# The opening of a conditioned decoder layer: c by DMA broadcast, eight early conditioning tiles, and a new order and pacing of the first weight pieces

## The chip, the cores and the metric

The kernel runs on one core of one Trainium2 chip. The metric is device time in microseconds for one execution, and for several runs their median. A core has TensorE (PE, matmuls), VectorE (DVE), ScalarE (ACT), GpSimd (POOL) and SyncE (SP, which here only issues DMAs); 16 DMA engines move data between HBM and the on-chip memory. Every engine works through its own queue in the order in which the program issued the instructions, and waits at an instruction until its inputs and its output buffer are ready.

## The reference, cut to what matters

One decoder layer on x (256 tokens by 2048) with a conditioning vector c (2048). Only the start of it is touched by the change:

```python
mod = (silu(c) @ w_cond + b_cond).reshape(B, 3, 3, 2048)
u = x * (1 + mod[:, 0, 1]) + mod[:, 0, 0]            # scale and shift of sub-layer 0
h = (silu(u @ ffn1_w1) * (u @ ffn1_w3)) @ ffn1_w2    # F = 5632
x = layer_norm(2**0.25 * x + 0.5 * (1 + mod[:, 0, 2]) * h)
...                                                  # mixer (attention | S5), then a second FFN
```

All values are fp32. w_cond has 9 x 2048 rows of 2048 numbers (75 MB), of which the scale and shift of the first FFN are 2 x 2048 rows.

## The kernel before, in words

**Conditioning pieces.** silu(c) lies in the tile `sc`, the same row on all 128 partitions. One *piece* is a tile `gv` of 128 rows by 1024 columns of w_cond (512 KB, `gv_load`, issued on SP at L211); `gv_step` multiplies it with half of `sc` on DVE and sums along the row into one column of `acc`. Four pieces (two blocks, shift and scale, by two halves) give the shift and scale for 128 columns of u, a *k-tile*. There are 16 k-tiles, grouped into four *units* of four; a unit is 16 pieces, so the first FFN needs 64 pieces (0 to 63), and later blocks the rest of 288. `gv` has four buffers (`GVB`), and a step loads up to three pieces ahead.

`finish` turns the sums into scale and shift (four small DVE operations); `modulate` makes the k-tile of u: ACT writes `uf` = scale * x + shift, then `Uh` (its rounded part, on ACT or DVE) and `Ul` = uf - Uh (DVE). For the first unit `finish` runs after every fourth piece; for later units, once after the sixteenth, through `gv_end`. x itself comes transposed in tiles `xT`, one per unit (`load_xT`).

**Weight pieces and jobs.** The FFN's weights come as tiles `raw` of 128 x 1024 (512 KB). A `Stream` holds a list of *jobs*, one weight piece each. For job j ACT writes hi(j) = rounded raw (`S.copy` in `split_to`), DVE writes lo(j) = raw - hi(j) (in `pay`), and PE multiplies in 12 matmuls of 512 columns (`form_b`): for each of two token tiles, hi with Uh and Ul of two k-tiles, then lo with Uh of both. `hi` and `lo` have four buffers each (`AHEAD`), `raw` four, of which three are used ahead from job 4 to job 51 (`RW`).

`Stream.run` issues, for each job, in this order: the job's `pre` functions, the matmuls, its `post` functions, what `later` has put on this job, the splits up to job j + `AHEAD` (ACT's hi and DVE's lo of job j + 4), and the job's background `bg`.

**The first 80 jobs** form u @ (w1 | w3) for five blocks b of 512 columns, for w1 and w3 (m = 0, 1), in four passes over k: pass i uses unit i. In each pass a block and m take two jobs, each with two k-tiles, so a pass has 20 jobs and starts at job 0, 20, 40, 60. The first job of each pass has in its `pre` a `gv_until`, which makes pieces until the unit is ready and then makes its four k-tiles of U at once. Blocks 0 to 3 are evicted from PSUM after each pass: in pass 0 by two ACT copies into a tile `kosum` per block and m (L909), in later passes by two DVE additions; block 4 stays in PSUM.

**The opening** (the end of `tile_layer`): c goes to one partition, four pairs of fp32 matmuls with a row of ones broadcast it into PSUM, and four Silu on ACT write `sc`. All 16 pieces of the first unit are made; the loads of the first weight pieces are slipped in after pieces 8 and 12 (`W0_AT`, the `NK` test), hi(0) after piece 13, and lo(0) to lo(3) after the last. Then the jobs run. Their background makes pieces up to a count that depends on the job:

```python
for i in range(4 * NT1):
    n = min(64, NK + math.ceil(min(i + 1, GA[0]) * GA[1] + max(0, i + 1 - GA[0]) * GA[2]))
    stream.q[i].bg.append(lambda n=n: steps(n - gv_n["done"]))
```

with GA = (20, 0.9, 0.8) and NK = 16. `lam_prep`, a chain of small DVE operations on four 64-vectors (`lamv`), is done after job 2. From job 80 on a planner (`drain`), which counts estimated PE and DVE time, puts the remaining pieces and the S5 preparation between the jobs.

Of the kernel before, what the change touches and what calls it, by code (L numbers as in the profile page):

```python
# [16 lines left out]
D = 2048  # L17
# [10 lines left out]
NSLAB = 12  # L28
GVB = 4
CH = 1024  # L30
DL = 2
DP = 0
RAW = 4
# [4 lines left out]
XA = 16  # L38
W0_AT = 12
S0_AT = 13  # L40
LIM = (2.6, 100.0, 100.0, 100.0)
# [3 lines left out]
GV_END = 256  # L45
GA = (20, 0.9, 0.8)
UNITS = ([("p", 0, q) for q in range(4)] + [("g", 2, h) for h in range(2)] + [("p", 3, q) for q in range(4)]
# [70 lines left out]
def tile_layer(tc, A, out):  # L118
    nc = tc.nc
    V, S, PE, SP, GP = Meter(nc.vector), nc.scalar, Meter(nc.tensor), nc.sync, nc.gpsimd  # L120
    with ExitStack() as ctx:
# [8 lines left out]
        def psum():  # L130
            return psp.tile([128, 512], F32, tag="ps", name="ps")
# [7 lines left out]
        def w1(shape, name):  # L139
            return small(shape, name, 5, tag="w1")  # L140
# [23 lines left out]
        sizes = {k: int(np.prod(v)) for k, v in shapes.items()}  # L164
        cst = sb.tile([128, sum(sizes.values())], F32, tag="cst", name="cst")
        SP.dma_start(cst, A["cst"])
        view, o = {}, 0
# [4 lines left out]
        bcT, lngT, lnbT, s5a, s5d, glub, sublng = (view[k] for k in shapes)  # L172
        lamv = w1([128, 4, 64], "lamv")
        SP.dma_start(lamv, A["lamv"].rearrange("(o a) b -> o a b", o=1).to_broadcast([128, 4, 64]))
        sc = sb.tile([128, D], F32, tag="sc", name="sc")
        SP.dma_start(sc[0:1, :], A["c"])
        ones = w1([1, 128], "ones")
        V.memset(ones, 1.0)
        for q in range(4):
            p = psum()  # L180
            PE.matmul(p, ones, sc[0:1, q * 512:(q + 1) * 512], start=True, stop=True)
            S.activation(sc[:, q * 512:(q + 1) * 512], p, AF.Silu)  # L182
        lam = sb.tile([128, 1], F32, tag="lam", name="lam")
# [7 lines left out]

        st = {"raw": RAW, "lim": None, "gv_max": 0.0, "gv_credit": 0.0, "s5_at": 0.0}

# [8 lines left out]
        def gv_load(k):  # L202
            while gv_n["load"] < min(k, len(gv_order), gv_n["cap"]):
                n = gv_n["load"]
                (kind, blk, i), j = gv_order[n]
                if kind == "p":
                    col, half = (blk + j % 2) * NK + 4 * i + j // 4, j // 2 % 2
                else:
                    col, half = blk * NK + 8 * i + j // 2, j % 2
                t = gvp.tile([128, 1024], F32, tag="gv", name="gv", bufs=GVB)  # L210
                SP.dma_start(t, A["w_cond"][col, :, half * 1024:(half + 1) * 1024])  # L211
                gv_tiles[n] = t, half
                gv_n["load"] += 1
# [391 lines left out]

        def lam_prep():
            pr = w1([128, 2, 64], "lampr")
            V.tensor_tensor(pr, lamv[:, 0:4:2, :], lamv[:, 1:4:2, :], op=ALU.mult)
            sm, ex = small([128, 2], "lams", 1), small([128, 2], "lame", 1)
            V.tensor_reduce(sm, pr, axis=AX.X, op=ALU.add)  # L610
            vexp(V, ex, sm, cells(w1([128, 256], "lamc")), 2)
            V.tensor_tensor(lam, ex[:, 0:1], ex[:, 1:2], op=ALU.subtract)
            V.tensor_scalar(lam, lam, LAMBDA_INIT, None, op0=ALU.add)


        class Stream:
# [43 lines left out]
            def run(self, n):  # L660
                for _ in range(n):
# [12 lines left out]
                    if not j.hold:  # L674
                        self.split_to(self.done + AHEAD)
                        for f in j.bg:
                            f()
                        drain()
# [200 lines left out]
        def ffn(w13, wd, blk, passes, tiles, kept):  # L879
# [138 lines left out]
            for i, (k0, k1) in enumerate(passes):  # L1018
                n = len(jobs)
                for b in range(tiles // 4):  # L1020
                    kps = range(k0 // 2, k1 // 2)
                    if (i, b) == (0, 0):
                        jobs += [mk_ko(i, b, m, kp) for kp in kps for m in range(2)]
                    else:
                        jobs += [mk_ko(i, b, m, kp) for m in range(2) for kp in kps]
                jobs[n].pre.append(lambda k0=k0, k1=k1: [gv_until("ready", blk, q) for q in range(k0 // 4, k1 // 4)])
            for pi, (f0, nf) in enumerate(PIECES):
# [414 lines left out]

        stream.limit = 0
        gv_load(2)
        load_xT(0)
        for n in range(NK):
            gv_step()
            if n + GVB == W0_AT:
                stream.limit = 10 ** 6
                stream.load_to(1)  # L1450
                stream.limit = 1
            if n + GVB == NK:
                stream.limit = 10 ** 6
                stream.load_to(RAW)
                gv_n["cap"] = len(gv_order)
            if n == S0_AT:
                stream.split_to(1, False)
        pay_late()
        stream.flush()
        stream.pay()  # L1460
        stream.split_to(AHEAD)
        for i in range(4 * NT1):
            n = min(64, NK + math.ceil(min(i + 1, GA[0]) * GA[1] + max(0, i + 1 - GA[0]) * GA[2]))
            stream.q[i].bg.append(lambda n=n: steps(n - gv_n["done"]))
# [126 lines left out]
```

## Time and profile before

| | us |
|---|---|
| runs (3) | median 1926.6, 1925.9 to 1926.9 |
| profiled execution | 1923.86 |
| its span, first to last instruction | 1921.6 |
| PE busy | 1853.3 (96%) |
| DVE busy | 1492.8 (78%) |
| ACT busy | 884.1 (46%) |
| DMA over the span | 532.35 MB, 277 GB/s |
| first matmul of the main work | 32.03 |
| start of unbroken matmuls | 40.69 |

All times in the trace count from the span's start. A row of a timeline gives start, duration, engine, line, operation, output tile and input tiles, and the shapes; in brackets stands how long the engine was idle before it and what released it. "x2" means that two instructions in a row were merged. L106 is a helper through which all DVE and PE calls pass, so rows are told apart by their tiles. A matmul's duration overlaps the next one's; the distance of the starts is its price.

### The profile page before, as it was taken

The numbers are of one execution on the slowest core, as the hardware profiler recorded it, in microseconds if no ns is written. First come the engines' busy times: TensorE is split into PE (matmuls) and PEld (weight loads), VectorE is DVE, ScalarE is ACT, GpSimd is POOL, SyncE is SP. The second block draws the span as 40 slices with busy tenths as digits, with TensorE's granted clock in tenths as the row PEclk, the third lists the DMA queues.
The fourth block names the chain that finished last, engine by engine and source line by source line (L and its number), as shares of the span: only waits on it lengthen the run. The fifth ranks groups of instructions, "written<-read, shape, count | busy, mean of one in ns | idle before, by whom it ended". The sixth has DMA issues, their size and how long they took to land.

```text
span 1921.6 us, 25394 instructions
## 1 busy us (share of the span) xinstructions
PE 1853.3 (96%) x9294; PEld 1559.2 (81%) x9294; DVE 1492.8 (78%) x2285; ACT 884.1 (46%) x1201; POOL 65.5 (3%) x119
## 2 busy tenths in 40 slices
PE   3999999999999999999999998999999999999997
PEld 2888887888888788889998886888888888888886
DVE  5999889788779878887998996888866555454568
ACT  2544544654553343544447635544444444334432
POOL 0000000000000000102210000000000000000000
PEclk9999999999999999999999998999999999999998
DMA  8999758998998898798989795998887655565563
GB/s 307 363 363 337 266 193 282 335 318 315 324 336 293 314 334 302 254 348 284 317 280 313 269 335 198 327 356 293 289 279 255 188 185 187 197 215 189 189 234 114
DMA packets 151791, 532.35 MB, mean 277 GB/s; under 512 B 21825, under 2 KB 23281, under 8 KB 150513
## 3 DMA queue, kind: packets, MB, share of 16 engines
q1 hardware_dynamic: 137090, 495.31, 74.5%
q0 software_dynamic: 6512, 23.89, 3.8%
q10 hardware_dynamic: 8064, 11.54, 1.7%
q8 instruction: 73, 1.20, 0.2%
q14 instruction: 52, 0.43, 0.1%
HBM read 513.34 MB, written 17.33 MB: 276 GB/s over the span
## 4 chain that ended last, share of the span: by engine, by line
PE 83%; DVE 9%; DMA 4%; ACT 2%; issue 2%; POOL 0%; SPq 0%; DVEq 0%; ACTq 0%
PE ps L106 83%; DVE lo L106 3%; DVE gv L106 3%; DMA raw<-in_f1w_dram 2%; DVE Y L106 1%; DMA gv<-in_w_cond_dram 1%; DVE cells L106 1%; ACT hi L647 1%; DMA scrB<-tabr 1%; DMA U<-sD 0%; DVE kosum L106 0%; ACT uf L696 0%; DMA raw<-in_f2w_dram 0%; ACT Y L818 0%; DVE st L106 0%
## 5 line engine op out<-in xcount | busy, mean ns | idle before, releaser
L106 DVE TENSOR_TENSOR lo<-raw,hi 128x1024 fp32r<-128x1024 f32 x630 | 766.1, 1221 | 332.5 <-ACT hi L647 328.9
L647 ACT CAST hi<-raw 128x1024 fp32r<-128x1024 f32 x630 | 660.6, 1052 | 705.0 <-PE ps L106 456.4
L106 PE MATMUL ps<-hi,Uh 128*128 128x512 f32 x1472 | 582.0, 395 | 22.7 <-ACT hi L647 21.7
L106 PE MATMUL ps<-hi,Ul 128*128 128x512 f32 x1472 | 576.4, 392 | 0.0
L106 PE MATMUL ps<-lo,Uh 128*128 128x512 f32 x1472 | 457.0, 392 | 8.0 <-DVE lo L106 8.0
L106 DVE SCALAR_TENSOR_TENSOR gv<-gv,sc 128x1024 f32<-128x1024 f32 x288 | 350.7, 1218 | 15.5 <-ACT sc L182 7.8
L106 PEld LDWEIGHTS ps<-hi,Uh 128*128 128x128 f32 x1472 | 278.0, 189 | 84.3 <-ACT hi L647 24.0
L106 PEld LDWEIGHTS ps<-lo,Uh 128*128 128x128 f32 x1472 | 277.5, 189 | 69.0 <-DVE lo L106 10.9
L106 PEld LDWEIGHTS ps<-hi,Ul 128*128 128x128 f32 x1472 | 278.3, 189 | 56.7 <-DVE Ul L106 0.5
L106 PE MATMUL ps<-hi,Hh 128*128 128x512 f32 (+1 forms) x716 | 274.9, 385 | 0.0
L106 PE MATMUL ps<-hi,Hl 128*128 128x512 f32 (+1 forms) x716 | 273.6, 383 | 0.0
L106 PE MATMUL ps<-lo,Hh 128*128 128x512 f32 (+1 forms) x716 | 216.9, 384 | 2.8 <-DVE lo L106 2.8
L106 PEld LDWEIGHTS ps<-lo,Hh 128*128 128x128 f32 x716 | 132.7, 188 | 31.0 <-DVE lo L106 4.7
L106 PEld LDWEIGHTS ps<-hi,Hh 128*128 128x128 f32 x716 | 134.5, 188 | 27.0 <-issue 0.8
L106 PEld LDWEIGHTS ps<-hi,Hl 128*128 128x128 f32 x716 | 134.6, 188 | 26.0
L106 PE MATMUL ps<-Uh,hi 128*128 128x256 f32 x384 | 98.6, 293 | 2.9 <-ACT sT L1076 1.8
L106 PE MATMUL ps<-Ul,hi 128*128 128x256 f32 x384 | 96.4, 288 | 0.2
L106 PEld LDWEIGHTS ps<-Uh,hi 128*128 128x128 f32 x384 | 74.8, 195 | 6.5 <-ACT sT L1076 2.7
L106 PEld LDWEIGHTS ps<-Ul,hi 128*128 128x128 f32 x384 | 74.9, 195 | 1.1 <-DVE Ul L106 1.0
L942 ACT CAST Hh<-ps 128x512 fp32r<-128x512 f32 x44 | 25.8, 587 | 87.6 <-PE ps L106 87.6
L106 DVE TENSOR_TENSOR Hl<-ps,Hh 128x512 fp32r<-128x512 f32 x44 | 30.2, 687 | 32.8 <-ACT Hh L942 32.8
L106 PE MATMUL ps<-Uh,lo 128*128 128x256 f32 x384 | 53.9, 283 | 0.0
(215 smaller groups left out, 1345.6 us busy)
## 6 DMA issues: line engine op xcount, KB each, us to landing
gv<-in_w_cond_dram SPq DMA_DIRECT2D x288, 512.0 KB, 6.7
raw<-in_f1w_dram SPq DMA_DIRECT2D x264, 512.0 KB, 5.9
raw<-in_f2w_dram SPq DMA_DIRECT2D x264, 512.0 KB, 4.7
raw<-in_win_a_dram SPq DMA_DIRECT2D x48, 512.0 KB, 6.2
raw<-in_wout_dram SPq DMA_DIRECT2D x32, 512.0 KB, 5.5
s5m<-scrB POOLq DMA_DIRECT2D x8, 1024.0 KB, 8.8
raw<-in_win_v_dram SPq DMA_DIRECT2D x16, 512.0 KB, 5.2
scrB<-s5f ACTq DMA_DIRECT2D x8, 640.0 KB, 10.6
```

Of the source, the lines that this page charges most:

```text
L106: return f(*a, **k)
L647: S.copy(hi, raw)
L942: S.copy(hh, p)
```

## The change

- c is read from HBM straight into all 128 partitions, in two transfers of 512 KB, and two Silu of 1024 columns work in place; the matmuls with ones go. A Silu on a tile of one column stands ahead of them.
- The first eight pieces (`EARLY`) lie in four of the twelve `slab` tiles instead of the `gv` ring, so that twelve pieces can be under way before the first step.
- Only eight pieces (k-tiles 0 and 1) are made before job 0, and only two jobs are split ahead (`st["split"]`) until job 4. Pieces 8 to 15 are made in the background of jobs 0 to 3, two each; the `pre` of job 4 sees to what is left and restores the distance of four.
- Pass 0 takes blocks 0 and 1 together, and all their jobs of k-tiles 0 and 1 (jobs 0 to 3) before those of k-tiles 2 and 3 (jobs 4 to 7).
- The pieces of the later units are paced by a new formula, counted from job 4.
- `lamv` is loaded after job 2, and its DVE work is put after job 8.

```diff
+EARLY = 8
...
-W0_AT = 12
-S0_AT = 13
...
-GA = (20, 0.9, 0.8)
+GA = (0.9, 0.8)
...
+        sc = sb.tile([128, D], F32, tag="sc", name="sc")
+        for h in range(2):
+            SP.dma_start(sc[:, h * 1024:(h + 1) * 1024], A["c"][:, h * 1024:(h + 1) * 1024].to_broadcast([128, 1024]))
         SP.dma_start(cst, A["cst"])
...
-        lamv = w1([128, 4, 64], "lamv")
-        SP.dma_start(lamv, A["lamv"].rearrange("(o a) b -> o a b", o=1).to_broadcast([128, 4, 64]))
-        sc = sb.tile([128, D], F32, tag="sc", name="sc")
-        SP.dma_start(sc[0:1, :], A["c"])
-        ones = w1([1, 128], "ones")
-        V.memset(ones, 1.0)
-        for q in range(4):
-            p = psum()
-            PE.matmul(p, ones, sc[0:1, q * 512:(q + 1) * 512], start=True, stop=True)
-            S.activation(sc[:, q * 512:(q + 1) * 512], p, AF.Silu)
+        one = w1([128, 1], "one")
+        V.memset(one, 1.0)
+        S.activation(one, one, AF.Silu)
+        for h in range(2):
+            S.activation(sc[:, h * 1024:(h + 1) * 1024], sc[:, h * 1024:(h + 1) * 1024], AF.Silu)
...
-                t = gvp.tile([128, 1024], F32, tag="gv", name="gv", bufs=GVB)
+                if n < EARLY:
+                    if n % 2 == 0:
+                        st["early"] = slab("early")
+                    t = st["early"][:, n % 2 * 1024:n % 2 * 1024 + 1024]
+                else:
+                    t = gvp.tile([128, 1024], F32, tag="gv", name="gv", bufs=GVB)
...
         def lam_prep():
+            lamv = w1([128, 4, 64], "lamv")
+            SP.dma_start(lamv, A["lamv"].rearrange("(o a) b -> o a b", o=1).to_broadcast([128, 4, 64]))
+            stream.later(6, lambda: lam_rest(lamv))
+
+        def lam_rest(lamv):
...
-                        self.split_to(self.done + AHEAD)
+                        self.split_to(self.done + st["split"])
...
-                for b in range(tiles // 4):
+                groups = [(0, 1), (2,), (3,), (4,)] if (i, blk) == (0, 0) else [(b,) for b in range(tiles // 4)]
+                for bs in groups:
                     kps = range(k0 // 2, k1 // 2)
-                    if (i, b) == (0, 0):
-                        jobs += [mk_ko(i, b, m, kp) for kp in kps for m in range(2)]
+                    if i == 0 and bs[0] == 0:
+                        jobs += [mk_ko(i, b, m, kp) for kp in kps for b in bs for m in range(2)]
                     else:
+                        b, = bs
                         jobs += [mk_ko(i, b, m, kp) for m in range(2) for kp in kps]
-                jobs[n].pre.append(lambda k0=k0, k1=k1: [gv_until("ready", blk, q) for q in range(k0 // 4, k1 // 4)])
+                if (i, blk) != (0, 0):
+                    jobs[n].pre.append(lambda k0=k0, k1=k1: [gv_until("ready", blk, q) for q in range(k0 // 4, k1 // 4)])
...
-        stream.limit = 0
-        gv_load(2)
+        gv_load(3)
         load_xT(0)
-        for n in range(NK):
+        gv_load(EARLY)
+        stream.load_to(2)
+        gv_load(EARLY + GVB)
+        for n in range(8):
             gv_step()
-            if n + GVB == W0_AT:
-                stream.limit = 10 ** 6
-                stream.load_to(1)
-                stream.limit = 1
-            if n + GVB == NK:
-                stream.limit = 10 ** 6
-                stream.load_to(RAW)
-                gv_n["cap"] = len(gv_order)
-            if n == S0_AT:
-                stream.split_to(1, False)
         pay_late()
-        stream.flush()
-        stream.pay()
-        stream.split_to(AHEAD)
+        stream.split_to(2)
+        gv_n["cap"] = len(gv_order)
+
+        def second():
+            steps(NK - gv_n["done"])
+            pay_late()
+            st["split"] = AHEAD
+        stream.q[4].pre.append(second)
         for i in range(4 * NT1):
-            n = min(64, NK + math.ceil(min(i + 1, GA[0]) * GA[1] + max(0, i + 1 - GA[0]) * GA[2]))
+            n = 8 + 2 * i + 2 if i < 4 else min(64, NK + math.ceil(min(i - 3, 16) * GA[0] + max(0, i - 19) * GA[1]))
             stream.q[i].bg.append(lambda n=n: steps(n - gv_n["done"]))
```

More of the change, by code (lines that the diff above doesn't have):

```diff
@@ L190, in tile_layer @@
         yD = dram.tile([1024, 4, 64], F32, tag="yD", name="yD")
-        st = {"raw": RAW, "lim": None, "gv_max": 0.0, "gv_credit": 0.0, "s5_at": 0.0}
+        st = {"raw": RAW, "split": 2, "lim": None, "gv_max": 0.0, "gv_credit": 0.0, "s5_at": 0.0}
         gv_order = [(u, kt) for u in UNITS for kt in range(NK)]
```

## The prediction

> **What bounds the kernel now.** I read the page's busy shares first, then stretches of the opening, then TensorE's own timeline.
>
> ```profile
> span 1921.6 us, 25394 instructions
> PE 1853.3 (96%) x9294; PEld 1559.2 (81%) x9294; DVE 1492.8 (78%) x2285; ACT 884.1 (46%) x1201; POOL 65.5 (3%) x119
> ```
>
> TensorE (PE) has work in flight for 1853 of 1922 us. A microsecond is therefore won or lost only where PE stands still. The stretches (columns: length, busy PE, weight loads, DVE, ACT, POOL, granted clock, DMA share, GB/s):
>
> ```profile
> 0.00:10.00 10.00, 4.32 (x5) 1.83 (x6) 0.32 (x2) 2.41 (x3) 1.59 (x9) 1.00 0.69 199
> 20.00:30.00 10.00, 0.00 (x0) 0.00 (x0) 8.45 (x21) 1.01 (x3) 0.00 (x0) 1.00 0.96 323
> 30.00:40.00 10.00, 2.08 (x4) 1.16 (x4) 6.62 (x15) 3.92 (x7) 0.00 (x0) 1.00 0.99 366
> 80.00:100.00 20.00, 20.00 (x90) 16.57 (x89) 18.05 (x31) 12.86 (x18) 0.00 (x0) 1.00 1.02 408
> 100.00:120.00 20.00, 20.00 (x90) 16.57 (x89) 20.00 (x27) 8.38 (x8) 0.00 (x0) 1.00 0.99 362
> ```
>
> PE is nearly idle for 40 us while the DMA engines are almost full, and from then on PE, DVE and DMA are all close to full together. PE's timeline:
>
> ```profile
> 32.03 0.80 PE L106 MATMUL ps<-hi,Uh 128*128 128x512 f32 x1 [19.19 <-ACT hi L647]
> 40.69 1.22 PE L106 MATMUL ps<-lo,Uh 128*128 128x512 f32 x2 [6.58 <-DVE lo L106]
> 41.70 0.63 PE L106 MATMUL ps<-hi,Uh 128*128 128x512 f32 x1
> 42.13 0.63 PE L106 MATMUL ps<-hi,Ul 128*128 128x512 f32 x1
> ...
> 44.08 0.40 PE L106 MATMUL ps<-hi,Uh 128*128 128x512 f32 x1
> 44.32 0.39 PE L106 MATMUL ps<-hi,Ul 128*128 128x512 f32 x1
> ...
> 95.77 0.39 PE L106 MATMUL ps<-hi,Uh 128*128 128x512 f32 x1
> ...
> 150.17 0.39 PE L106 MATMUL ps<-hi,Uh 128*128 128x512 f32 x1
> ...
> 205.66 0.39 PE L106 MATMUL ps<-hi,Uh 128*128 128x512 f32 x1
> ```
>
> Job 1 begins at 44.08, job 20 at 95.77, job 40 at 150.17, job 60 at 205.66. (95.77 − 44.08)/19 = 2.72 us a job, so job 4 began at 44.08 + 3 × 2.72 = 52.24. Between jobs 20 and 40 nothing is lost (20 × 2.72 = 54.4); between 40 and 60 it is 55.49 − 54.4 = 1.1. Jobs 20, 40 and 60 each need four new columns of U. How close that is today, in DVE's and ACT's order at the first of these places:
>
> ```profile
> 90.31 1.22 DVE L106 TENSOR_TENSOR lo<-raw,hi 128x1024 fp32r<-128x1024 f32 x1
> 91.45 1.22 DVE L106 SCALAR_TENSOR_TENSOR gv<-gv,sc 128x1024 f32<-128x1024 f32 x1
> 92.59 0.08 DVE L106 DVE_READ_ACCUMULATOR gv<-gv,sc 128x1 f32 x1
> 92.70 0.17 DVE L106 SCALAR_TENSOR_TENSOR gs<-acc 128x4 f32<-128x4 f32 x1
> ...
> 93.18 1.09 ACT L696 ACTIVATE uf<-xT,bt,gs 128x256 f32<-128x256 f32 x2 [3.08 <-DVE bt L106]
> 93.81 0.29 DVE L106 CAST Uh<-uf 128x256 fp32r<-128x256 f32 x1 [0.67 <-ACT uf L696]
> 94.14 0.43 DVE L106 TENSOR_TENSOR Ul<-uf,Uh 128x256 fp32r<-128x256 f32 x1
> 94.31 0.41 ACT L698 CAST Uh<-uf 128x256 fp32r<-128x256 f32 x1
> ...
> 97.13 1.23 DVE L106 TENSOR_TENSOR lo<-raw,hi 128x1024 fp32r<-128x1024 f32 x1 [0.53 <-ACT hi L647]
> ```
>
> Here lo(20), conditioning piece 31, then Uh(4) complete at 94.10, 1.7 us before job 20 wants it. From these starts: a lo or a piece takes 1.14 us in sequence; from the start of a unit's last piece to the end of its first Uh it is 94.10 − 91.45 = 2.65.
>
> **The opening, part by part.** The eight broadcast matmuls (L181) and four Silu reading PSUM go. Today the first piece starts behind them:
>
> ```profile
> 3.20 0.15 DVE L106 TENSOR_SCALAR g<-cst 128x1 f32<-128x1 f32 x1 [2.21 <-DMA cst<-in_cst_dram]
> 10.10 1.23 DVE L106 SCALAR_TENSOR_TENSOR gv<-gv,sc 128x1024 f32<-128x1024 f32 x1 [6.74 <-ACT sc L182]
> gv<-in_w_cond_dram SPq DMA_DIRECT2D x288, 512.0 KB, 6.7
> gb<-in_lng_dram SPq DMA_DIRECT2D x6, 512.0 KB, 7.1
> ```
>
> c now comes as two 512 KB transfers, the shape of gb (one row to 128 partitions), which lands like any other transfer of that size (7.1 against 6.7 us). With 366 GB/s (the 30 to 40 stretch) one transfer of 0.524 MB takes 1.43 us; cst's landing at 3.2 with 0.18 MB puts the start of the flow at 2.7. In queue order: c twice, cst (0.34 of a transfer), three pieces, xT, five pieces, two weight pieces (raw 0, 1), four pieces, raw 2, raw 3. SP issues these 20 in about 20 × 0.42 = 8 us, none behind a buffer. Piece 0 lands at 2.7 + 3.34 × 1.43 = 7.5, the last early one at 18.9; the Silu work (two of 1024 columns, about 1.1 us each like ACT's casts) and its table load lie under the 7.5. So the first step starts 2.6 us earlier, but the eighth only at 18.9: DMA is the limit, and c's own megabyte costs 2.9 us of it. Piece 7, finish, uf, Uh and hi(0) put job 0 near 22.7, instead of 32.03.
>
> That start is not what counts; job 4 is, since it needs columns 2 and 3, which are pieces 8 to 15. They stand on DVE behind lo(2), and raw 2 lands behind 18.34 transfers, at 2.7 + 18.34 × 1.43 = 28.9. DVE has lo(0), lo(1) done by 25.1 and waits, with pieces 8 to 11 already there. From 28.9: hi(2) 1.15; lo(2), 8, 9, lo(3), 10, 11 6 × 1.14 + 0.1; finish 0.48; uf, Uh, hi(4) on ACT 2.1 (hi(4) stands behind uf(2)); lo(4), 12, Ul(2), 13, lo(5), 14, 15 7.3; finish 0.48; uf and Uh(3) 1.0. Sum 19.4, so Uh(3) at 48.3. Jobs 0 to 3 end by about 36.5, so PE then waits some 12 us. Two of job 4's matmuls run before (−0.45); the clock adds 1.4 (below). **Job 4 starts in effect at 49.25, 3.0 us earlier than 52.24.** Bounds by DMA rate: 408 GB/s puts raw 2 at 26.4, 323 GB/s at 32.4: gain 5.5 to a loss of 0.5.
>
> A sentence apart on this rate: the Trainium skill, "DMA: Bandwidth & Descriptors", section "Two cost components", has bytes/436 GB/s, by which, as an estimate, raw 2 would land at 24.8 and the gain be 7.1; no stretch quoted here reaches it.
>
> lamv and its DVE work move from job 2 to job 8:
>
> ```profile
> 51.98 0.28 DVE L106 TENSOR_TENSOR lampr<-lamv 128x128 f32<-128x128 f32 x1
> ...
> 55.88 0.15 DVE L106 TENSOR_SCALAR lam<-lam 128x1 f32<-128x1 f32 x1
> 54.72 1.05 ACT L647 CAST hi<-raw 128x1024 fp32r<-128x1024 f32 x1 [0.73 <-PE ps L106]
> 54.97 0.39 PE L106 MATMUL ps<-hi,Uh 128*128 128x512 f32 x1
> L909 ACT COPY kosum<-ps x16: 573/588/593, 48.6 to 85.4; 128x512 f32<-128x512 f32 x16
> ```
>
> 3.9 us on DVE, covered by lo(9) to lo(11), which are done by then; uncovered it would be a 3.9 us stall. The lamv transfer behind its two neighbours on SP is 128 KB, nothing. The early slabs are free until the kosum and H tiles ask, and four of twelve are handed back by piece 7.
>
> **The pacing, which decides.** Today the background of job i brings the piece count to 16 + ceil(0.9(i+1)): 32 after job 16, three jobs ahead of job 20. The new line gives 16 + ceil(0.9 × 16) = 31 after job 19; 16 + ceil(14.4 + 0.8 × 20) = 47 after job 39; 16 + ceil(14.4 + 0.8 × 40) = 63 after job 59. A unit is complete at 32, 48, 64. So at each of the three boundaries the last piece is missing by one and is made by gv_until in the `pre` of jobs 20, 40, 60, after everything that earlier jobs put on DVE: lo(23) and piece 30 among it. lo(23) and hi(23) use the buffers of job 19 (four of each), so they can't start before PE has read those. The last rows show that wait: hi(8) at 54.72, 0.25 us before PE's next job at 54.97. With T the end of job 19:
>
> hi(23) T − 0.25 to T + 0.8; lo(23) from T + 0.9; piece 30 from 2.04; piece 31 from 3.18; Uh(4) 2.65 later, at T + 5.83; PE reads it at about **T + 5.9**. Behind that chain wait, on DVE and ACT, lo(24) and hi(24), which want job 20 anyway; on SP raw 27 and piece 34, three and four ahead of use. PE has nothing else: job 20 is next in its order. Nothing covers it.
>
> After such an idle PE starts slowly:
>
> ```profile
> 644.01 0.33 PE L106 MATMUL ps<-ident,sg 128*128 128x128 f32 x1 [3.42 <-DVE sg L106]
> 645.16 0.78 PE L106 MATMUL ps<-hi,Uh 128*128 128x512 f32 x1
> ...
> 646.16 0.63 PE L106 MATMUL ps<-hi,Uh 128*128 128x512 f32 x1
> 646.59 0.63 PE L106 MATMUL ps<-hi,Ul 128*128 128x512 f32 x1
> ...
> 648.17 0.40 PE L106 MATMUL ps<-hi,Ul 128*128 128x512 f32 x1
> 644.00:648.00 4.00, 3.72 (x11) 2.96 (x12) 4.00 (x6) 1.53 (x2) 0.00 (x0) 0.57 0.93 301
> ```
>
> Seven intervals from 645.16 to 648.17 take 3.0 us where 0.227 each (2.72/12) would be 1.6: 1.4 us more, granted clock 0.57. A stall costs 5.9 + 1.4 = **7.3**. On this the Trainium skill, "TensorE: Matmul & The Clock Gate", section "Part 1: The HAM clock gate", says that idling through a window of about 3.4 us halves the clock until about 3.4 busy us have passed; by it, as an estimate, a stall loses 1.7 to the clock instead of 1.4, 0.9 us more over three; the row after 3.42 us of idle agrees with it within that.
>
> Is DVE able to keep PE's pace up to job 19? From lo(6), which waits on ACT for job 4's two evictions (job 4 ends at 52.0, the second eviction takes 0.59, hi(6) 1.05, so lo(6) starts at 53.9): 18 lo and 15 pieces 33 × 1.14 = 37.6, lam 3.9, then 2.75: Uh(4) at 98.2. By PE: 49.25 + 16 × 2.72 + 5.9 = 98.7. They agree; DMA needs 63 transfers by then, 2.7 + 63 × 1.43 = 92.8, so it isn't last. In the later passes PE's chain is longer than DVE's, because the stall lets DVE catch up.
>
> **The sum.** Job 20: 98.7 + 1.4 = 100.1 against 95.77, +4.3. Job 40: +7.3 = +11.6. Job 60: +7.3 − 1.1 (today's loss there) = +17.8. From job 61 on both kernels have the same instructions in the same order, and PE is full, so it stays. The profiled execution was 1923.86 (span 1921.6 and 2.3 around it): 1941.7. The runs' median lies 2.7 above that execution; the median forecast is 1926.6 + 17.8 = **1944**.
>
> **Rivals.** (a) *The chain is partly covered.* Only the last piece's 2.65 + 0.1 stands open, with no slow clock, because lo(23) and piece 30 turn out to be done in time: 3 × 2.75 − 3.0 − 1.1 = +4.2, 1931. For: DVE often idles for raw tiles. Against: the four buffers. (b) *Faster: no boundary stall.* DVE's order at the three boundaries would have to put the unit's last piece before lo(23), in front of PE's end of job 19; then the chain (5.8 us) fits into jobs 18 and 19 and the opening's 3.0 us, up to 5.5, survive: 1924 to 1921. It decides from the point where Uh(4) is ready before job 19 ends. For: today's trace has no stall there and the new pacing takes three pieces (3.4 us of DVE) out of the jobs before. Against: DVE's order in the rows above is that of the program. (c) *The opening loses too.* If the flow ramps as in today's first 10 us (199 GB/s against 366 from 2.7 on leaves 0.7 MB, 1.9 us) and c's transfers land late, the 3.0 becomes a loss of about 2, and DMA makes each boundary a microsecond or so later: 1944 + 5 + 3 = 1952.
>
> **Chances.** Forecast 0.70 (own range 1937 to 1949: three stalls of 5.9 to 8.0 with the opening's bounds), (a) 0.10, (b) 0.10, (c) 0.10. About 0.2% (3.9 us) is what runs of this kernel can tell from no change. (b) gives 0.08 faster and 0.02 same, (a) half same and half slower, the rest slower: 0.08, 0.07, 0.85. Range 1931 to 1952: it leaves out (b) and the tail beyond (c).
>
> **What would show it.** PE idle before jobs 20, 40 and 60, each about 6 us, released by Uh, followed by seven or eight matmuls spaced 0.43; DVE with lo, piece, piece, four small operations in front of it; first main matmul near 23 and a second idle of 12 us that ends near 48; DVE idle from 25 to 30 for hi(2). Wrong if no idle over 2 us stands at those boundaries, or if job 4 starts before 46.

## The result, and the profile after

The changed kernel takes 1952.0 us (median of four runs, 1949.6 to 1954.0) where the kernel before takes 1926.8 on the same chip: slower, ratio 1.0132 with an interval of 1.0118 to 1.0147. The forecast was 1944 with a range of 1931 to 1952; the median, 1952.02, lies at the far end and just beyond it. So the sign and the mechanism came out and the size didn't. The profiled execution is the longest of the four, 1953.97. Its page, busy shares:

```profile
span 1951.7 us, 25360 instructions
PE 1858.2 (95%) x9286; PEld 1565.9 (80%) x9286; DVE 1494.6 (77%) x2285; ACT 884.8 (45%) x1200; POOL 64.0 (3%) x119
```

The span grew by 30 us and PE's busy time by 5. The rest is standing still, and PE's timeline shows where (the helper that was L106 is L105 in the changed kernel and L107 in e9_early12; ACT's hi is L654):

```profile
22.53 0.80 PE L105 MATMUL ps<-hi,Uh 128*128 128x512 f32 x1 [22.53 <-ACT hi L654]
...
48.01 0.80 PE L105 MATMUL ps<-hi,Uh 128*128 128x512 f32 x1 [6.35 <-ACT Uh L295]
...
53.68 0.39 PE L105 MATMUL ps<-hi,Ul 128*128 128x512 f32 x1
...
93.37 0.61 PE L105 MATMUL ps<-lo,Uh 128*128 128x512 f32 x2
101.89 0.79 PE L105 MATMUL ps<-hi,Uh 128*128 128x512 f32 x1 [7.91 <-DVE Uh L105]
...
104.94 0.40 PE L105 MATMUL ps<-hi,Ul 128*128 128x512 f32 x1
...
157.34 0.61 PE L105 MATMUL ps<-lo,Uh 128*128 128x512 f32 x2
163.62 0.79 PE L105 MATMUL ps<-hi,Uh 128*128 128x512 f32 x1 [5.67 <-DVE Uh L105]
...
169.72 0.39 PE L105 MATMUL ps<-hi,Uh 128*128 128x512 f32 x1
...
228.63 0.80 PE L105 MATMUL ps<-hi,Uh 128*128 128x512 f32 x1 [7.47 <-DVE Uh L105]
...
234.66 0.39 PE L105 MATMUL ps<-hi,Uh 128*128 128x512 f32 x1
```

The idles of 7.91, 5.67 and 7.47 stand before jobs 20, 40 and 60, released by the first Uh of the unit, and 6.35 before job 4. The rows without a bracket at 53.68, 104.94, 169.72 and 234.66 are the first at the full spacing again: 13, 7, 14 and 14 intervals after the stalls, in 5.67, 3.05, 6.10 and 6.03 us. At 0.227 each these would be 2.95, 1.59, 3.18 and 3.18, so the slow clock costs 2.7, 1.5, 2.9 and 2.9. Job 4, counted as in the prediction, starts at 48.01 − 0.45 = 47.56, 4.7 before the old 52.24.

An idle counts from the modelled end of the last matmul, 0.39 after its start, though its price is 0.227; a stall is therefore the idle and 0.16: 8.1, 5.8 and 7.6. The stretches (columns as in the prediction):

```profile
20.00:30.00 10.00, 7.47 (x25) 6.06 (x26) 4.55 (x10) 5.00 (x6) 0.00 (x0) 1.00 1.03 408
...
50.00:60.00 10.00, 10.00 (x38) 8.11 (x37) 5.72 (x7) 7.01 (x10) 0.00 (x0) 0.82 0.31 97
80.00:100.00 20.00, 13.98 (x62) 11.26 (x60) 18.61 (x25) 8.34 (x9) 0.00 (x0) 0.95 1.02 406
163.60:171.60 8.00, 7.98 (x23) 6.25 (x24) 3.91 (x7) 2.98 (x6) 0.00 (x0) 0.62 0.29 112
```

DVE, which had 8.45 of 10 us to do from 20 to 30, now has 4.55; the DMA engines are busy for less than a third of the time from 50 to 60 (0.31) and full again from 80 on (1.02). (The conditioning weights are more than the 75 MB named above: 288 pieces of 512 KB are 151 MB.) DVE's timeline, with the opening and the three boundaries:

```profile
28.66 1.23 DVE L105 TENSOR_TENSOR lo<-raw,hi 128x1024 fp32r<-128x1024 f32 x1 [3.79 <-ACT hi L654]
...
54.27 3.50 DVE L105 TENSOR_TENSOR lo<-raw,hi 128x1024 fp32r<-128x1024 f32 x3 [5.86 <-ACT hi L654]
...
61.97 1.23 DVE L105 TENSOR_TENSOR lo<-raw,hi 128x1024 fp32r<-128x1024 f32 x1 [0.77 <-ACT hi L654]
...
66.12 1.23 DVE L105 SCALAR_TENSOR_TENSOR gv<-gv,sc 128x1024 f32<-128x1024 f32 x1 [0.62 <-DMA gv<-in_w_cond_dram]
...
84.98 1.22 DVE L105 TENSOR_TENSOR lo<-raw,hi 128x1024 fp32r<-128x1024 f32 x1 [1.06 <-ACT hi L654]
...
95.75 1.22 DVE L105 SCALAR_TENSOR_TENSOR gv<-gv,sc 128x1024 f32<-128x1024 f32 x1
...
96.89 1.22 DVE L105 TENSOR_TENSOR lo<-raw,hi 128x1024 fp32r<-128x1024 f32 x1
...
158.62 1.23 DVE L105 TENSOR_TENSOR lo<-raw,hi 128x1024 fp32r<-128x1024 f32 x1 [0.34 <-ACT hi L654]
159.76 1.22 DVE L105 SCALAR_TENSOR_TENSOR gv<-gv,sc 128x1024 f32<-128x1024 f32 x1
...
160.91 1.22 DVE L105 SCALAR_TENSOR_TENSOR gv<-gv,sc 128x1024 f32<-128x1024 f32 x1
...
222.96 1.22 DVE L105 SCALAR_TENSOR_TENSOR gv<-gv,sc 128x1024 f32<-128x1024 f32 x1
...
225.91 1.23 DVE L105 SCALAR_TENSOR_TENSOR gv<-gv,sc 128x1024 f32<-128x1024 f32 x1 [1.72 <-DMA gv<-in_w_cond_dram]
```

Job 40 is the forecast chain to a tenth. The last two matmuls of job 39 start at 157.34 and are over, at 0.227 each, at T = 157.79; lo(43) starts at T + 0.83 (forecast 0.9), piece 46 at T + 1.97 (2.04), piece 47 at T + 3.12 (3.18), and PE goes on at T + 5.83 (5.9). Before job 60 the same chain waits 1.72 more for piece 63. Its load was issued three pieces ahead, but only at 218.02, 6.2 us before DVE was free for it, and took 7.9 us. The buffer that it needed (piece 59's) had been free since 214.4; on SP the load stood behind two weight loads that took from 215.56 to 217.97.

Before job 20, lo(23) starts at 96.89, behind the piece at 95.75 and with no idle in front: DVE is late by itself. T there is 93.37 + 0.45 = 93.8, so lo(23) is at T + 3.1 and not T + 0.9. From the start of lo(6) to that of lo(23) the forecast had 31 steps of 1.14 and lam's 3.9, 39.2 us; it took 42.6 (54.27 to 96.89). Of the 3.4 us more, 2.6 are waits of DVE, for which the forecast had no term: 0.77, 1.06 and 0.19 for an hi, each of which had itself waited on ACT for its weight piece to land, and 0.62 for a conditioning piece.

### The profile page after: what moved, and what is told of

The parts are those of the page before. It is cut to its first block, busy times and chain, and to the rows that moved or that the text cites. A ratio compares the mean times of both kernels' runs of the same rounds, so it can differ in the third digit from the quotient of the medians.

```text
span 1951.7 us, 25360 instructions
## 1 busy us (share of the span) xinstructions
PE 1858.2 (95%) x9286; PEld 1565.9 (80%) x9286; DVE 1494.6 (77%) x2285; ACT 884.8 (45%) x1200; POOL 64.0 (3%) x119
## 4 chain that ended last, share of the span: by engine, by line
PE 86%; DVE 7%; DMA 4%; ACT 1%; issue 1%; POOL 0%; SPq 0%; DVEq 0%; ACTq 0%
PE ps L105 86%; DVE lo L105 2%; DVE gv L105 2%; DMA raw<-in_f1w_dram 1%; DVE Y L105 1%; DVE cells L105 1%; DMA gv<-in_w_cond_dram 1%; DMA U<-sD 1%; DMA early<-in_w_cond_dram 1%; DMA scrB<-tabr 1%; DMA raw<-in_win_a_dram 1%; ACT hi L654 0%; ACT uf L703 0%; DMA cst<-in_cst_dram 0%; ACT Y L825 0%
## 5 line engine op out<-in xcount | busy, mean ns | idle before, releaser
L105 DVE TENSOR_TENSOR lo<-raw,hi 128x1024 fp32r<-128x1024 f32 x630 | 767.1, 1222 | 358.0 <-ACT hi L654 351.7
L654 ACT CAST hi<-raw 128x1024 fp32r<-128x1024 f32 x630 | 661.5, 1053 | 726.4 <-PE ps L105 530.7
L105 PE MATMUL ps<-hi,Uh 128*128 128x512 f32 x1472 | 586.6, 399 | 55.6 <-ACT hi L654 27.7
L105 PE MATMUL ps<-hi,Ul 128*128 128x512 f32 x1472 | 580.4, 394 | 2.2 <-DVE Ul L105 2.2
L105 PE MATMUL ps<-lo,Uh 128*128 128x512 f32 x1472 | 459.5, 394 | 1.4 <-DVE lo L105 1.4
L105 PEld LDWEIGHTS ps<-hi,Uh 128*128 128x128 f32 x1472 | 280.7, 191 | 117.2 <-ACT hi L654 28.3
L105 DVE SCALAR_TENSOR_TENSOR gv<-gv,sc 128x1024 f32<-128x1024 f32 x280 | 340.9, 1219 | 5.5 <-DMA gv<-in_w_cond_dram 5.3
L105 PEld LDWEIGHTS ps<-lo,Uh 128*128 128x128 f32 x1472 | 279.5, 190 | 62.4 <-DVE lo L105 3.1
L105 PEld LDWEIGHTS ps<-hi,Ul 128*128 128x128 f32 x1472 | 280.8, 191 | 60.2 <-DVE Ul L105 3.4
L105 PE MATMUL ps<-hi,Hh 128*128 128x512 f32 (+1 forms) x716 | 274.9, 385 | 0.0
L105 PE MATMUL ps<-hi,Hl 128*128 128x512 f32 (+1 forms) x716 | 273.6, 383 | 0.0
L105 PE MATMUL ps<-lo,Hh 128*128 128x512 f32 (+1 forms) x716 | 216.9, 384 | 2.7 <-DVE lo L105 2.7
L105 PEld LDWEIGHTS ps<-lo,Hh 128*128 128x128 f32 x716 | 132.7, 188 | 30.9 <-DVE lo L105 4.8
L105 PEld LDWEIGHTS ps<-hi,Hh 128*128 128x128 f32 x716 | 134.6, 188 | 27.0 <-issue 0.8
L105 PEld LDWEIGHTS ps<-hi,Hl 128*128 128x128 f32 x716 | 134.6, 188 | 26.0
L105 PE MATMUL ps<-Uh,hi 128*128 128x256 f32 x384 | 98.9, 294 | 3.7 <-ACT sT L1086 2.9
L105 PE MATMUL ps<-Ul,hi 128*128 128x256 f32 x384 | 96.7, 288 | 0.1
L105 PEld LDWEIGHTS ps<-Uh,hi 128*128 128x128 f32 x384 | 75.1, 196 | 7.4 <-ACT sT L1086 3.7
L105 PEld LDWEIGHTS ps<-Ul,hi 128*128 128x128 f32 x384 | 74.9, 195 | 0.9 <-DVE Ul L105 0.7
L105 DVE TENSOR_TENSOR Hl<-ps,Hh 128x512 fp32r<-128x512 f32 x44 | 30.3, 688 | 34.5 <-ACT Hh L949 34.5
L105 PE MATMUL ps<-Uh,lo 128*128 128x256 f32 x384 | 53.9, 283 | 0.0
```

The source lines that it names most:

```text
L105: return f(*a, **k)
L654: S.copy(hi, raw)
```

## The experiments

Each kernel ran beside the kernel before on the same chip (medians 1924.3 to 1925.5); the ratio is against that. Diffs are against the changed kernel where nothing else is said.

**The pacing alone** (e2_pace_only; against the kernel before).

```diff
-            n = min(64, NK + math.ceil(min(i + 1, GA[0]) * GA[1] + max(0, i + 1 - GA[0]) * GA[2]))
+            n = min(64, NK + math.ceil(max(0, min(i - 3, 16)) * 0.9 + max(0, i - 19) * 0.8))
```

> The kernel before with the new pacing alone: no pieces during jobs 0 to 3, then 31, 47 and 63 done after jobs 19, 39 and 59; opening, c and job order as before. Theory P: three idles of 5.5 to 8 us at jobs 20, 40 and 60, each followed by 3 to 6 us at half clock (1.4 to 2.9 us lost), 1946 to 1953. Rival D: the opening is the old one, so nothing or next to nothing is lost, 1925 to 1929.

1948.6 us (1947.2 to 1949.8), ratio 1.0126 [1.0109, 1.0143]. PE's timeline of it:

```profile
100.79 0.79 PE L106 MATMUL ps<-hi,Uh 128*128 128x512 f32 x1 [5.93 <-DVE Uh L106]
...
162.95 0.80 PE L106 MATMUL ps<-hi,Uh 128*128 128x512 f32 x1 [5.67 <-DVE Uh L106]
...
225.97 0.80 PE L106 MATMUL ps<-hi,Uh 128*128 128x512 f32 x1 [6.87 <-DVE Uh L106]
```

One line of the pacing, in the old kernel with its old opening, costs 23.8 us: nearly the whole loss. Job 20's idle is 5.93 here and not 7.91, so the two extra microseconds there come with the rest of the change.

**The units complete three jobs ahead** (e1_lead3), as before the change, with the rest of the change kept.

```diff
-... NK + math.ceil(min(i - 3, 16) * GA[0] + max(0, i - 19) * GA[1]))
+... NK + math.ceil(min(i - 3, 13) * 16 / 13 + max(0, i - 16) * GA[1]))
```

> The changed kernel with one line different: the pieces of units 1, 2 and 3 are complete three jobs ahead of jobs 20, 40 and 60, as in the kernel before. Theory P (pacing: the missing piece stands behind lo(23) and thus behind the end of job 19): the idles before jobs 40 and 60 (5.7 and 7.5 us in the changed kernel) shrink to under 1 us; the one before job 20 (7.9 us) to about 4.5, since three lo of 1.14 us no longer stand ahead of it but DVE is late there anyway; the time comes to 1929 to 1933. Rival D (DMA: the megabyte of the broadcast c and the deep early prefetch make weight and conditioning pieces late in all of pass 0 to 2): the three idles stay above 5 us each, 1947 to 1953.

1934.9 us (1933.0 to 1940.7), 1.0062 [1.0041, 1.0083]. PE's timeline:

```profile
74.72 0.74 PE L105 MATMUL ps<-lo,Uh 128*128 128x512 f32 x2 [2.19 <-DVE lo L105]
...
99.21 0.50 PE L105 MATMUL ps<-hi,Uh 128*128 128x512 f32 x1 [1.73 <-DVE Uh L105]
...
156.50 0.50 PE L105 MATMUL ps<-hi,Uh 128*128 128x512 f32 x1 [0.58 <-ACT hi L654]
...
213.43 0.50 PE L105 MATMUL ps<-hi,Uh 128*128 128x512 f32 x1 [0.80 <-ACT hi L654]
```

The stalls before jobs 40 and 60 are gone, and 17 us with them. Still it is 10 us slower than the kernel before, a little more than expected. One new stall stands at 74.72, where DVE is behind PE after a wait of 2.64 us for a conditioning piece at 65.99 (0.62 in the changed kernel). That the 16 pieces now asked of 13 jobs cause it isn't shown: e5_lead1 below asks 16 of 15 jobs and has the same (a wait of 2.87, then 2.44 of idle at 75.03), and e12_fill_lead3, at the pace of e1_lead3 but with the pieces loaded earlier, has neither.

**One job ahead** (e5_lead1): the units complete after jobs 18, 38 and 58.

```diff
+... NK + math.ceil(min(i - 3, 15) * 16 / 15 + max(0, i - 18) * 0.78))
```

> The changed kernel with each unit complete one job ahead (after jobs 18, 38 and 58) instead of none. Between the changed kernel (idles 5.7 and 7.5 us at jobs 40 and 60) and the version three jobs ahead (under 1 us). Theory P, as the last runs have it (each place earlier in the order starts the chain one gate, 2.72 us, earlier, and one piece less stands in it): idle at jobs 40 and 60 of 2 us where the piece has landed, up to 4 where it is late; at job 20 4 to 6; mostly too short for the full slow clock; 1936 to 1943. If the stall is all or nothing, either the 1952 of the changed kernel or the 1935 of three jobs ahead.

1939.7 us (1938.3 to 1943.8), 1.0084 [1.0058, 1.011]. Timeline of PE, then two stretches of 8 us behind equal idles:

```profile
102.30 0.79 PE L105 MATMUL ps<-hi,Uh 128*128 128x512 f32 x1 [4.50 <-DVE Uh L105]
...
160.84 0.51 PE L105 MATMUL ps<-hi,Uh 128*128 128x512 f32 x1 [1.81 <-DVE Uh L105]
...
219.14 0.50 PE L105 MATMUL ps<-hi,Uh 128*128 128x512 f32 x1 [1.81 <-DVE Uh L105]
```

```profile
161.00:169.00 8.00, 8.00 (x28) 6.30 (x29) 6.90 (x12) 4.83 (x7) 0.00 (x0) 0.79 0.81 299
219.00:227.00 8.00, 7.86 (x33) 6.17 (x34) 6.75 (x11) 6.17 (x10) 0.00 (x0) 1.00 0.72 266
```

The price is graded, as the chain says: one job of lead took 3.86 off the idle of 5.67 before job 40, which is one gate (2.72) and one piece less in the chain (1.14). By the same step two jobs would leave nothing; that was not run, and three (e1_lead3) left 0.58 and 0.80.

**The last piece ahead of lo(23)** (e4_before_lo): the order of rival (b).

```diff
+        for q in (1, 2, 3):
+            stream.q[20 * q - 1].post.append(lambda q=q: gv_until("ready", 0, q))
```

> The changed kernel with the same counts of pieces, but what is missing of a unit and its four k-tiles of U are made in the post of jobs 19, 39 and 59, so in front of lo(23), lo(43), lo(63) in DVE's and ACT's order instead of behind them. Theory P: the chain no longer starts at PE's end of the job; the idles before jobs 40 and 60 shrink to 0 to 2 us, the one before job 20 by one lo, to about 6.8, as DVE is late there by itself; 1930 to 1937. If the count itself or DMA lateness is the cause, the idles stay: 1947 to 1953.

1951.0 us (1949.6 to 1951.0), 1.0139 [1.0124, 1.0154]: no gain clear of the noise, against the expectation. DVE's timeline before job 40, and ACT's for the hi in front of it:

```profile
156.96 1.23 DVE L105 TENSOR_TENSOR lo<-raw,hi 128x1024 fp32r<-128x1024 f32 x1 [0.35 <-ACT hi L654]
158.10 1.22 DVE L105 SCALAR_TENSOR_TENSOR gv<-gv,sc 128x1024 f32<-128x1024 f32 x1
...
159.24 1.22 DVE L105 SCALAR_TENSOR_TENSOR gv<-gv,sc 128x1024 f32<-128x1024 f32 x1
...
161.00 1.23 DVE L105 SCALAR_TENSOR_TENSOR gv<-gv,sc 128x1024 f32<-128x1024 f32 x1 [0.52 <-DMA gv<-in_w_cond_dram]
```

```profile
155.87 1.05 ACT L654 CAST hi<-raw 128x1024 fp32r<-128x1024 f32 x1 [1.67 <-PE ps L105]
```

lo(43) no longer stands in the chain, but lo(42) does, gated in the same way by the end of job 38. That gate opens 2.7 us earlier. Behind it stand three pieces in a row where there were two (1.14 more), and the third is then late by 0.52, before job 60 by 2.08. The idle before job 40 falls only to 4.71. Moved forward by one place in an in-order queue, the task still stands behind the previous gate.

**lam, the first suspect for the lateness at job 20** (e6_lam_late): its DVE work moved behind the first FFN's passes.

```diff
-        stream.q[2].post.append(lam_prep)
+        stream.q[62].post.append(lam_prep)
```

> The changed kernel with lamv's load and its 3.9 us of DVE work after jobs 62 and 68 instead of 2 and 8. Theory L (DVE is 2.2 us late at job 19's end because of lam): the idle before job 20 falls from 7.9 to between 5.7 and 6.2 us, the others stay, 1947 to 1951. Rival R (DVE is late there because ACT waits for weight pieces from DMA, about 1.5 us a job): the idle before job 20 stays at 7.5 to 8, 1949 to 1954.

1952.1 us (1950.7 to 1954.0), 1.0146 [1.0117, 1.0174]; the idle before job 20 is 7.89 as ever. The theory falls, and the forecast that lam is covered at job 8 holds: with its 3.9 us gone lo(23) starts at 96.08, only 0.8 earlier, and DVE's waits between lo(6) and lo(23) grow from 2.6 to 5.0. DVE goes there at the pace at which pieces land.

**The clock** (e7_warm): in the `pre` of jobs 20, 40 and 60, behind the unit's DVE work and ahead of the job, PE does 20 matmuls whose products nobody uses.

```diff
+                if blk == 0 and i:
+                    def warm():
+                        p = psum()
+                        for _ in range(20):
+                            PE.matmul(p, kx(st["U"][0], 0, 0, 128), st["U"][0][0][:, 0:512], start=True, stop=True)
+                    jobs[n].pre.append(warm)
```

> The changed kernel with 20 matmuls of 512 columns on finished data (their product is not used) in front of the wait at jobs 20, 40 and 60, so that PE idles some 4.5 us less and the wait for U stays where it is. Theory C (of the 27 us that the three boundaries cost, 7 to 8 are the half clock after the idle: 1.4, 2.9, 2.9): the following matmuls are spaced 0.227 us at once, Uh is ready at the same time, and the time falls by 5 to 8: 1944 to 1948. Rival: the clock falls anyway in the 1 to 3 us that remain, or the extra matmuls delay job 20, and the time stays, 1950 to 1955.

1950.8 us (1949.1 to 1953.6), 1.014 [1.0115, 1.0164]. PE's timeline at job 40 (the 20 matmuls run from 157.58 for 4.70 us) and the stretches after the three stalls:

```profile
163.41 0.51 PE L105 MATMUL ps<-hi,Uh 128*128 128x512 f32 x1 [1.14 <-DVE Uh L105]
```

```profile
101.00:109.00 8.00, 7.95 (x26) 6.08 (x27) 4.09 (x8) 3.66 (x7) 0.00 (x0) 0.79 0.47 179
163.40:171.40 8.00, 7.99 (x33) 6.25 (x34) 5.63 (x9) 4.04 (x7) 0.00 (x0) 1.00 0.49 174
225.40:233.40 8.00, 7.99 (x27) 6.32 (x28) 4.24 (x8) 3.86 (x7) 0.00 (x0) 0.79 0.27 99
```

The clock after the second stall is whole where the changed kernel had 0.62; after the other two, with 3.17 and 2.37 of idle left, it is not. The expected 1944 to 1948 didn't come, and the median didn't settle the theory, so this kernel and the changed one ran once more side by side.

> The changed kernel again, beside the next one on the same chip: 1949 to 1954, with half-rate matmuls after the idles at jobs 20, 40 and 60.

> The changed kernel with 20 matmuls in front of the three waits, again. In its first profile the idles were 3.2, 1.1 and 2.4 us and the clock stayed up only after the 1.1; 4.2 us were gone by the end of the 80 jobs. Theory C: 2 to 5 us less than the run beside it. Rival: no difference beyond 1 us.

1951.2 us (1950.4 to 1955.4) for the changed kernel and 1948.3 (1946.4 to 1950.8) with the matmuls: 2.9 us less, within the expectation and about one stall's clock, as only one stall was short enough (1.14, clock 1.00; the others 4.18 and 2.97, clock 0.65 and 0.61 in the 8 us behind them). But the ranges of the two overlap by 0.4, so the medians lean towards the theory and don't prove it; that the slow clock follows the stalls is read from the traces.

**c by DMA, alone** (e3_bcast_only; against the kernel before) **and undone** (e10_c_matmul). The first puts the new loading of c and its two Silu into the old kernel, the second the old four matmul pairs into the new one.

> The kernel before with the broadcast of c by DMA alone (two transfers of 512 KB, a Silu ahead for the table, no matmuls with ones). Theory P: the first step on DVE comes 2 us earlier, the DMA engines carry 1 MB more (about 2.5 us) before the weight pieces; the two about cancel: unbroken matmuls start at 39.5 to 42.5, 1925 to 1929. Rival D: the megabyte delays all that DMA feeds and DMA has no slack up to 200 us, so the full 2.5 us or more show: 1929 to 1934.

> The changed kernel with the old way of c: 8 KB to one partition and matmuls with ones. Of the new opening this takes 1 MB out of the DMA queue (2.5 us) and starts DVE 2 us later, at about 10. Theory P: job 4's Uh(3) comes 1 to 2.5 us earlier than in the changed kernel (47.6), the three idles stay; 1948 to 1952. Rival D (the megabyte is what makes everything late): the idles shrink too, under 1945.

Alone: 1927.0 us (1924.6 to 1930.6), 1.0016 [1.0005, 1.0027]; the unbroken matmuls start at 42.05 in place of 40.69. Undone: 1953.0 (1952.1 to 1953.9), 1.0146 [1.0127, 1.0166]; job 4 starts 0.8 earlier, and the idle before job 20 is 9.05. The time undone is a microsecond above what was expected (1948 to 1952). The megabyte costs a microsecond at the start and isn't what makes job 20 late.

**Pieces before splits in jobs 0 to 3** (e8_order), with three jobs of lead and lam at job 68.

```diff
-                        self.split_to(self.done + st["split"])
-                        for f in j.bg:
-                            f()
+                        if st["split"] < AHEAD:
+                            for f in j.bg:
+                                f()
+                            self.split_to(self.done + st["split"])
+                        else: ...
```

> The changed kernel with three edits: units complete three jobs ahead, lam late (jobs 62 and 68), and in jobs 0 to 3 the two pieces go before the split of the next job, so that DVE does pieces 8 and 9, which have landed, while raw 2 is still on its way. Theory P with the opening's own loss (DVE stands 4 to 5 us before lo(2) and is late in all of pass 0): job 4 starts at 46 to 48 instead of about 50, no idle over 1 us at jobs 20, 40, 60; 1921 to 1926, at or below the kernel before. If instead DMA bounds the opening, the reordering gives nothing: job 4 at 49 to 51, and about 1931.

1933.4 us (1931.1 to 1936.8), 1.0049 [1.0032, 1.0066]: a miss. PE's timeline:

```profile
44.71 0.80 PE L105 MATMUL ps<-hi,Uh 128*128 128x512 f32 x1 [4.44 <-ACT Uh L295]
47.25 0.80 PE L105 MATMUL ps<-hi,Ul 128*128 128x512 f32 x1 [1.75 <-DVE Ul L105]
```

Job 4's third matmul starts at 44.71, 3.3 us earlier than in the changed kernel, but its fourth waits for Ul until 47.25. Counted from there job 4 starts at 47.25 − 0.68 = 46.57, 1.0 us earlier. Job 20 starts at 95.62 behind 2.34 of idle, not clearly earlier than the old 95.77. lam in its new place costs an idle of 2.12 at 243.46.

**The gap in the DMAs filled** (e11_fill): pieces 16 to 23 lie in slabs too, so that their loads go out at job 4, into the empty 50 to 60.

```diff
-                if n < EARLY:
+                if n < EARLY or 16 <= n < 24:
...
         def second():
+            gv_load(24)
```

> The changed kernel, with pieces 16 to 23 also in the early slabs (free again by then) and their loads issued at job 4 instead of one by one. In the changed kernel DMA is busy to 0.31 (97 GB/s) between 50 and 60 us, as all its target buffers are full, and to 1.02 between 80 and 100, where ACT waits for weight pieces. Theory F (that gap is what makes DVE 2 us late at job 19): DMA share between 50 and 60 us over 0.8, idle before job 20 from 7.9 to 5.7 to 6.5 us, the others as they were, 1948 to 1951. Rival: DVE is late by its own work, the idle stays at 7.5 to 8.5, 1950 to 1954.

1950.8 us (1950.1 to 1953.0), 1.0141 [1.0126, 1.0156]. The stretches:

```profile
50.00:60.00 10.00, 10.00 (x36) 7.96 (x36) 5.02 (x6) 6.90 (x10) 0.00 (x0) 0.77 0.85 325
80.00:100.00 20.00, 14.84 (x66) 11.96 (x64) 18.06 (x23) 7.74 (x9) 0.00 (x0) 0.97 1.02 400
```

The gap is closed (0.85 against 0.31), lo(23) starts at 96.44 instead of 96.89, and the idle before job 20 is 7.08 instead of 7.91, between the two expectations. From lo(6) to lo(23) it now takes 41.5 us (54.98 to 96.44) where it took 42.6. But the DMA engines are as full from 80 on as before, and job 4 starts 0.7 later. Job 20 starts at 101.92: what is won at the stall is lost ahead of it.

**The same with three jobs of lead** (e12_fill_lead3), the best that the new opening gave.

> The same with units complete three jobs ahead. If pacing and the DMA gap were all that was wrong with the new opening, no idle over 1 us is left at jobs 20, 40 and 60 and the opening's 2 to 3 us show: 1921 to 1925. If DVE and DMA still bound jobs 4 to 60, small idles remain and it lies between: 1926 to 1932.

1930.6 us (median of ten, 1925.9 to 1933.7), 1.0028 [1.0015, 1.004]. PE's timeline:

```profile
96.44 0.50 PE L105 MATMUL ps<-hi,Uh 128*128 128x512 f32 x1 [2.04 <-DVE Uh L105]
```

Job 4 starts 4.5 us before that of the kernel before (48.20 − 0.45 against 52.24), and job 20 0.7 after it. The gain goes in two places: 14 slow intervals behind job 4's wait cost 2.9, and the stall before job 20 costs 2.04 + 0.16. With pacing and gap mended the new opening is still not faster.

**The early slabs alone** (e9_early12; against the kernel before). The old order, the old pacing and the old matmuls for c stay; twelve pieces lie in slabs, so all 16 loads and the four raw loads go out at once.

```diff
+EARLY = 12
...
+                if n < EARLY:
+                    if n % 2 == 0:
+                        st["early"] = slab("early")
+                    t = st["early"][:, n % 2 * 1024:n % 2 * 1024 + 1024]
+                else:
+                    t = gvp.tile([128, 1024], F32, tag="gv", name="gv", bufs=GVB)
...
+        gv_load(NK)
+        stream.load_to(RAW)
+        gv_n["cap"] = len(gv_order)
```

> The kernel before with the early slabs alone, twelve instead of eight: all 16 pieces of the first unit and the four first weight pieces are issued at once; c by matmuls, all 16 pieces before job 0, job order and pacing as before. Theory P (in the opening DMA was held back by four buffers, 297 to 323 GB/s between 10 and 30 us; the pacing did the damage): DMA runs at about 400 GB/s there, the 16 steps go through at 1.2 us each from 10.1 to about 31, unbroken matmuls start at 32 to 35 instead of 40.7, and 3 to 7 us stay: 1917 to 1922. Rival B (DVE and DMA together bound jobs 0 to 60, so an earlier start is given back as idles before job 60): matmuls start early, idles of the same size follow by job 60, 1923 to 1927.

**1918.5 us** (median of twelve, 1915.5 to 1922.6) against 1924.3, ratio 0.9968 [0.9956, 0.998]: faster than both kernels. Its stretches and the last idle of PE before the transposes of `kosum`, which start at 218.0 instead of 225.1:

```profile
10.00:20.00 10.00, 2.07 (x3) 0.33 (x1) 8.93 (x20) 2.20 (x4) 0.00 (x0) 1.00 1.03 415
20.00:30.00 10.00, 0.00 (x0) 0.00 (x0) 9.93 (x25) 2.06 (x5) 0.00 (x0) 1.00 1.02 409
```

```profile
34.58 1.22 PE L107 MATMUL ps<-lo,Uh 128*128 128x512 f32 x2 [1.45 <-DVE lo L107]
```

The flow is 409 to 415 GB/s where the old opening has 323 from 20 to 30, DVE is busy for 9.93 of 10 us from 20 to 30, and the unbroken matmuls start 6.1 us earlier, a gain that stays. The slabs and the earlier issue of the weight loads came in one edit; which of the two gives how much is open.

## Why the prediction was right about the sign and short of the size

The steps, in the prediction's order, forecast and measured (us, with sign as a loss against the kernel before; from the rows of the changed kernel above):

| step | forecast | measured |
|---|---|---|
| job 4, start | −4.4 | −4.7 |
| job 4, slow clock | +1.4 | +2.7 |
| job 20, stall + slow clock | 5.9 + 1.4 | 8.1 + 1.5 |
| job 40, stall + slow clock | 5.9 + 1.4 | 5.8 + 2.9 |
| job 60, stall + slow clock, less the old 1.1 | 5.9 + 1.4 − 1.1 | 7.6 + 2.9 − 1.1 |
| sum | +17.8 | +25.7 |

The sum agrees with the measured 25.3 of the medians, and with a mark behind all of this, the first eviction into Y, in the groups of the kernel before and of the changed one:

```profile
L973 ACT COPY Y<-ps x4: 579/587/592, 285.4 to 310.5; 128x512 f32<-128x512 f32 x4
```

```profile
L980 ACT COPY Y<-ps x2: 589/589/589, 310.8 to 312.1; 128x512 f32<-128x512 f32 x2
```

It moved by 25.4. The other 4.7 of the profiled execution's 30.1 came later; executions of the changed kernel lie about 5 us apart (after_again, 1950.4 to 1955.4), so they can't be put down to the change. For the same reason the sum is good to a few microseconds only: in after_again's profile the same steps are −4.9 + 1.5, 8.4 + 2.3, 5.8 + 1.8 and 6.9 + 2.6 − 1.1, in sum +23.3.

- **What held.** The pacing leaves each unit one piece short, the piece stands behind a lo that waits for PE's last job, and nothing covers it: e2_pace_only shows it alone, e1_lead3 and e5_lead1 take it away by degrees, and the chain at job 40 is right to 0.1. The opening is right up to job 4: first main matmul at 22.53 (22.7 forecast), job 4 at 48.01 (48.3), with DVE waiting for hi(2) until 28.66.
- **What failed: the price "5.9 + 1.4 = 7.3" of a stall, and the same 1.4 at job 4.** Of the 7.9 us missing, 4.4 are the clock (1.3 + 0.1 + 1.5 + 1.5). The 1.4 was read from one place, with seven slow intervals; three of four places here had 13 or 14, and after_again had 7, 12, 8 and 12. The place that was read also has four small transposes, from 644.01 on, in the same stretch of clock 0.57, which the seven leave out. On this the Trainium skill, "TensorE: Matmul & The Clock Gate", section "Part 1: The HAM clock gate", says that the window runs free and that one kernel can show 6, 11 or 14 slow matmuls at its start from run to run. The traces agree that the count varies (7 to 14 behind these idles). A term taken from a single event should have had bounds; by these rows they are 1.4 to 3.
- **"They agree", at 98.2 for DVE and 98.7 for PE, was the second failure:** +2.2 at job 20. Two chains that end within half a microsecond are not one covered by the other. The step that failed is "DMA needs 63 transfers by then, 2.7 + 63 × 1.43 = 92.8, so it isn't last": the sum had DVE at work from lo(6) to lo(23) without a wait, and the rows show 2.6 us of waits for tiles that come by DMA, enough for the 2.2. e2_pace_only puts the lateness down to the rest of the change and not the pacing; lam (e6_lam_late) and c's megabyte (e10_c_matmul) are ruled out. Filling the DMA gap shortens that stretch from 42.6 to 41.5 us, and lo(23) stands at T + 1.8 there, so about half of the 2.2 belongs to the gap. Why pieces land late in the other half stays open.
- **The third: raw 27 and piece 34 were counted as queued with room to spare, but no term held a late piece 63:** 1.72 at job 60, as its load stood on SP behind weight loads that waited for their own buffers.
- **The rivals.** (a) and (b) fell: three idles stand there, and e4_before_lo shows that (b)'s order would not have saved them. (c) named 1952, the time measured, but largely by luck: the loss that it saw up to job 4 didn't come (job 4 is 4.7 earlier), while its lateness of DMA at the boundaries did come, at two of the three (2.2 and 1.7); the clock, which it didn't name, made up the rest.
- **Where the opening's gain would have gone without the stalls** was not asked. e12_fill_lead3 and e8_order answer it: job 4 is 4.5 and 5.7 us earlier, the slow clock behind its wait costs 2.9 and 3.0, the stall before job 20 costs 2.2 and 2.5, and job 20 is 0.7 later and 0.15 earlier. So half or more of the gain goes to a restart of PE that the early start brings with it: PE starts, runs out of U at job 4 and has to start again. The rest goes to DVE and the DMA engines, which are full before job 20 and have the pieces put off from the opening to do; that these pieces are the cause is likely, but no run shows it alone. The kernel e9_early12, which puts none off, keeps 6 us.

## What to carry to other kernels

A task that an in-order engine gets "just in time" waits for everything in front of it; find the instruction ahead of it that is gated by a buffer, and complete the task earlier by more than its whole chain (here 5.8 us: one job of lead left 1.8 us of idle, three left under 1). An opening is ahead only if all its work is done by the later mark, so compare kernels where nothing is put off any more, and count the restart after an early start that has to wait again. Price a restart of TensorE with a range, and read it from several idles.

## What the runs showed of the hardware that was not expected

- The same idle of 1.81 us, twice in one execution of e5_lead1, was followed once by a granted clock of 0.79 and once by 1.00. Among the other short idles, 1.14 (e7_warm), 2.04 (e12_fill_lead3) and 2.34 (e8_order) kept the clock at 1.00 in the 8 us behind them, and 1.73 (e1_lead3) and 2.37 (e7_warm) were followed by 0.79. So a gap under 2 us can already lose it, and a longer idle doesn't mean a longer recovery: 7 slow intervals after 7.91 us, 14 after 5.67.
- With enough transfers under way the DMA engines moved 406 to 415 GB/s over 10 to 20 us, where the prediction took 366 from the old opening; e9_early12, with more loads issued at once, has 415 and 409 from 10 to 30, where the kernel before has 297 and 323. So the old opening was short of transfers in flight, not of bandwidth.
